# First four weight tiles of an encoder layer regrouped by quarters of the contraction, and the row statistics moved to ScalarE

## The chip, the cores and the metric

One core of one Trainium2 chip runs the whole program. The number compared is the device time of one execution in microseconds (us). The engines are TensorE (PE, matmuls; its weight loads are listed as PEld), VectorE (DVE), ScalarE (ACT), GpSimd (POOL) and SyncE (SP), which here only issues DMA loads and stores.

## The reference, cut to what matters

One layer of an encoder on 256 tokens of width 2048, in float32. The part that the change touches is its beginning: an RMS norm of x and the first columns of one wide input projection.

```python
def rms_norm(x, g):
    xf = x.astype(jnp.float32)
    y = xf * lax.rsqrt(jnp.mean(xf * xf, axis=-1, keepdims=True) + NORM_EPS)
    return (y * g.astype(jnp.float32)).astype(x.dtype)

h = rms_norm(x, norm_g[l])
proj = h @ w_in[l]              # 2048 x 24576
a_qkv, a_gate, b_in, b_gate, c_qkv, c_gate, merge = jnp.split(proj, SPLITS, axis=-1)
# three branches A (dilated attention), B (long convolutions), C (differential attention),
# each times silu of its gate, projected, merged by sigmoid gates, then one output projection
out = ... branches @ w_proj, merged, @ w_out, final rms_norm
```

## The kernel before, in words

All weights are read once, as a stream of tiles of 128 partitions x 2048 floats (1 MB). One tile is one *unit* of work; `_plan` lists the units in order: sixteen gate units (eight for branch A, eight for B), then convolution columns, attention columns, and so on. A gate unit is 128 output columns of `w_in` with the whole contraction of 2048, which is 16 chunks of 128 rows. A unit gets one accumulator in PSUM (tile `acc`, four buffers), 512 wide: TensorE keeps the weights of a chunk still and moves the 256 tokens past them.

Float32 accuracy is made from a split: every operand is a high part (rounded to fp32r) and a low part (the rest). ScalarE makes the high part (`nc.scalar.copy`, L177), VectorE subtracts it to get the low part (L178); both work on half a weight tile at a time (`split_half`), which gives `hl`, four buffers, two tiles' worth. For each chunk TensorE then issues two matmuls: high weights against [x high, x low] side by side, 512 columns (L705), and low weights against x high, 256 columns (L707). I call the two a *pair*; a gate unit is 16 pairs. `half_b` (L729) and `summed` (L737) add the two halves of the accumulator when the unit is done: ScalarE copies one half out, VectorE adds the other.

The order on each engine is the order in which the code issues (manual schedule), so the loop `for i in range(NU)` fixes it. In round i come the end of the units before (`evs`), the split of tile i+1, the load of tile i+3 (`raw`, three buffers, all on SyncE's queue), and the matmuls of unit i in two halves; between the halves a step of a background task (`step`) may run.

The start is special. x comes in transposed (`xt`, four loads of four chunks each, 512 KB) between the halves of the first weight tile. The norm's factor per token (`rstd`) isn't known yet, so the first sixteen units use x*g without it (`xg`, L268 for the high halves on ScalarE, L269 for the low ones on VectorE), and their results are multiplied by `rstd` at the end (L751). GpSimd squares the four x tiles (L238) and adds them in pairs (L240), VectorE adds the rest (`stats_sum`, L278), one matmul with ones sums over the partitions (`stats_rstd`, L283, between the halves of unit 2), ScalarE takes the root (L285) and VectorE the reciprocal (L286). Before the first data TensorE runs 18 and then 4 matmuls on ones (`warm_up`, L228), with the two products of the bias strips between them (L233). GpSimd issues the loads of the small constants (`const`, L217): two ahead of its squares, ten behind them. In rounds 3 and 4 the results of units 0 and 1, then 2 and 3, are taken out of their accumulators.

Of the kernel before, what the change touches and what calls it, by code (L numbers as in the profile page):

```python
# [10 lines left out]
F32 = mybir.dt.float32  # L11
# [4 lines left out]
S = 256  # L16
# [17 lines left out]
def _plan():  # L34
    """The weight stream: one entry per 128 x 2048 tile."""
# [45 lines left out]


def _stream(w_in, w_proj, w_out):
# [69 lines left out]
def trunk_kernel(ctx: ExitStack, tc: tile.TileContext, A, out, dbg=None):  # L153
# [17 lines left out]
    def split_half(i, h):  # L171
        if i >= NU:
            return
        t = base.tile([128, 2, 1024], F32R, name=f"hl{i}_{h}", tag="hl", bufs=4)
        hl[i, h] = t
        src = raw[i][:, 1024 * h:1024 * h + 1024]
# [12 lines left out]
    # ---------------------------------------------------------------- start  # L189
# [8 lines left out]
    nc.scalar.dma_start(norm_g, A["norm_g"])  # L198
    raw[0] = base.tile([128, 2048], F32, name="raw0", tag="raw", bufs=3)
    xt = []  # L200
    for c in range(4):
        t = k4(f"xt{c}", [128, 4, 256])
        nc.sync.dma_start(t, A["xT"][:, 4 * c:4 * c + 4, :])
        xt.append(t)
        if c in (0, 2):
            h = slice(512 * c, 512 * c + 1024)
            nc.sync.dma_start(raw[0][:, h], A["ws"][0][:, h])
# [11 lines left out]

    oh = slab("oh", [35, 768])  # L220
# [11 lines left out]
    for j in range(2):
        nc.tensor.matmul(ps_strip[:, j, 0:384], tabl, oh[:, 384 * j:384 * j + 384], start=True, stop=True)  # L233
    warm_up(4)
    sq = [k4(f"sq{j}", [128, 4, 256]) for j in range(2)]
    sq += [slab(f"sq{j}", [128, 4, 256]) for j in (2, 3)]
    for c in range(4):
# [10 lines left out]
    ident = const("ident", [128, 128])  # L248
# [10 lines left out]
    # x * g, split; its tokens' scale (rstd) is applied to the first products, and to hT  # L259
    xg = []  # L260
    for c in range(4):
        for k in range(4):
            if k % 2 == 0:
                t = slab(f"xg{c}_{k}", [128, 2, 512], F32R)
                xg.append(t)
            g = norm_g[:, 4 * c + k:4 * c + k + 1]
            o = t[:, k % 2]
            nc.scalar.activation(o[:, 0:256], xt[c][:, k], AF.Copy, scale=g)  # L268
            nc.vector.scalar_tensor_tensor(o[:, 256:512], xt[c][:, k], g, o[:, 0:256].bitcast(F32),  # L269
                                           op0=OP.mult, op1=OP.subtract)  # L270
        if c % 2 == 0:
            split_half(0, c // 2)
# [3 lines left out]
    def stats_sum():  # L276
        for a, b in ((sq[0], sq[2]), (sq[0][:, 0:2], sq[0][:, 2:4]), (sq[0][:, 0], sq[0][:, 1])):
            nc.vector.tensor_tensor(a, a, b, op=OP.add)  # L278
        return sq[0][:, 0]
# [26 lines left out]
    # ------------------------------------------------- bias strips and filters' hidden layer  # L306
# [12 lines left out]
    def sine(ps, j, name):  # L319
        """sin(freq * (ps + b)) with the argument brought into [-pi, pi]."""  # L320
# [31 lines left out]
    # ---------------------------------------------------------------- B: long convolutions  # L352
# [12 lines left out]
    def forward(xh, xl, zname):  # L365
        """[c of even, s of even, c of odd, s of odd] -> [Zr, Zr', S, D]."""
# [54 lines left out]
    def spectra(z, g, nm):  # L421
        """Z, G -> [Pc, Pv, Mc, Mv]."""
# [57 lines left out]
    # ---------------------------------------------------------------- A: dilated attention  # L480
# [71 lines left out]
    # ---------------------------------------------------------------- C: differential attention  # L552
# [103 lines left out]
    # ---------------------------------------------------------------- branches, split for the projections  # L656
# [16 lines left out]
    # ---------------------------------------------------------------- the units of the weight stream  # L673
# [269 lines left out]
    for i in range(NU):  # L943
# [44 lines left out]
        for e in evs:  # L988
            next(e, None)
# [100 lines left out]
```

## Time and profile before

| what | value |
|---|---|
| timed runs | 1432.51, 1432.66, 1433.47 us; median 1432.66 |
| profiled execution, span from first to last instruction | 1432.1 us; no time of its own is listed beside the span |
| TensorE busy | 1415.3 us, 99% |
| VectorE, ScalarE, GpSimd busy | 965.2 us, 730.0 us, 53.1 us |
| mean granted TensorE clock | 0.994 of full |
| DMA | 260.36 MB, mean 182 GB/s |

The busy share is a mean over 1432 us: a few us of waiting in one place hardly show in it. To see them one asks what TensorE waited for, and then for the timeline of that stretch. The granted clock is a share of full speed (1.0 is 2.4 GHz, 0.5 is 1.2 GHz).

### The profile page before, as it was taken

How to read it: one execution, taken by the hardware profiler on the slowest of the kernel's cores; microseconds unless marked ns; L12 is line 12 of the kernel's file. 1: busy time of each engine (PE TensorE's matmuls, PEld its weight loads, DVE VectorE, ACT ScalarE, POOL GpSimd, SP SyncE). 2: the span in 40 equal slices, each digit the busy share in tenths (PEclk: the TensorE clock that was granted, in tenths of full speed). 3: DMA queues.
4: the chain of work that ended last, by engine and by line, in shares of the span. 5: the costliest groups of instructions: out<-in, count | busy, mean ns of one | idle time of the engine just before them, and what ended most of it. 6: DMA issues, size and time to landing. Idle time of an engine off the chain costs nothing.

```text
span 1432.1 us, 20342 instructions
## 1 busy us (share of the span) xinstructions
PE 1415.3 (99%) x8134; PEld 1239.4 (87%) x8134; DVE 965.2 (67%) x1374; ACT 730.0 (51%) x1150; POOL 53.1 (4%) x74
## 2 busy tenths in 40 slices
PE   7999999999999999999999999999999999999997
PEld 5888899889988888889888888888888888888886
DVE  7787677676766676676655576775666666666554
ACT  4655545444445444454455576775454554545443
POOL 5000000000000000000000000000000000000000
PEclk8999999999999999999999999999999999999999
DMA  7655445454544445554455545444555556554552
GB/s 256 201 187 188 177 178 171 157 186 174 173 176 157 183 175 171 166 180 171 150 189 188 185 169 188 161 174 177 184 198 177 181 200 251 206 191 177 206 192 102
DMA packets 39870, 260.36 MB, mean 182 GB/s; under 512 B 5315, under 2 KB 5342, under 8 KB 10464
## 3 DMA queue, kind: packets, MB, share of 16 engines
q1 hardware_dynamic: 34992, 246.43, 48.0%
q0 software_dynamic: 4064, 11.58, 3.3%
q8 instruction: 64, 1.05, 0.3%
q10 hardware_dynamic: 720, 1.06, 0.2%
q14 instruction: 30, 0.25, 0.0%
HBM read 256.85 MB, written 2.20 MB: 181 GB/s over the span
## 4 chain that ended last, share of the span: by engine, by line
PE 98%; DVE 1%; DMA 1%; issue 0%; ACT 0%; SPq 0%; DVEq 0%
PE acc L705 48%; PE acc L707 24%; PE acc L722 6%; PE acc L723 6%; PE acc L721 6%; DMA xt<-in_xT 1%; PE ps_ef L407 1%; PE ps_o L473 0%; PE av L546 0%; PE lg L502 0%; DVE xg L269 0%; PE ps_fZ L356 0%; PE ps_fZ L355 0%; PE ps_fG L355 0%; PE ps_fZ L354 0%
## 5 line engine op out<-in xcount | busy, mean ns | idle before, releaser
L705 PE MATMUL acc<-hT,hl 128*128 128x512 f32 x2304 | 815.3, 397 | 0.0
L178 DVE TENSOR_TENSOR hl<-raw,hl 128x1024 fp32r<-128x1024 f32 x464 | 561.6, 1223 | 147.5 <-ACT hl L177 137.5
L707 PE MATMUL acc<-hT,hl 128*128 128x256 f32 x2304 | 646.3, 280 | 0.0
L705 PEld LDWEIGHTS acc<-hT,hl 128*128 128x128 f32 x2304 | 432.3, 188 | 100.4 <-issue 0.3
L177 ACT CAST hl<-raw 128x1024 fp32r<-128x1024 f32 x464 | 480.1, 1050 | 72.2 <-PE acc L723 51.8
L707 PEld LDWEIGHTS acc<-hT,hl 128*128 128x128 f32 x2304 | 435.4, 189 | 0.4
L729 ACT COPY eb<-acc 128x256 f32<-128x256 f32 x176 | 65.2, 371 | 294.1 <-PE acc L707 292.4
L705 PE MATMUL acc<-bhl,hl 128*128 128x512 f32 x384 | 135.1, 392 | 0.0
L721 PE MATMUL acc<-hl,hT 128*128 128x512 f32 (+1 forms) x320 | 111.3, 348 | 0.0
L722 PE MATMUL acc<-hl,hT 128*128 128x512 f32 (+1 forms) x320 | 111.1, 347 | 0.0
L723 PE MATMUL acc<-hl,hT 128*128 128x512 f32 (+1 forms) x320 | 111.1, 347 | 0.0
L707 PE MATMUL acc<-bhl,hl 128*128 128x256 f32 x384 | 108.4, 282 | 0.0
L705 PE MATMUL acc<-xg,hl 128*128 128x512 f32 x256 | 93.4, 405 | 5.3 <-DVE xg L269 5.3
L705 PEld LDWEIGHTS acc<-bhl,hl 128*128 128x128 f32 x384 | 72.1, 188 | 15.7
L737 DVE TENSOR_TENSOR mg<-acc,eb 128x256 f32<-128x256 f32 x48 | 20.3, 423 | 84.0 <-ACT eb L729 84.0
L707 PE MATMUL acc<-xg,hl 128*128 128x256 f32 x256 | 73.9, 289 | 1.5 <-DVE hl L178 1.5
L707 PEld LDWEIGHTS acc<-bhl,hl 128*128 128x128 f32 x384 | 72.5, 189 | 0.0
L723 PEld LDWEIGHTS acc<-hl,hT 128*128 128x128 f32 x320 | 60.6, 189 | 7.6
L721 PEld LDWEIGHTS acc<-hl,hT 128*128 128x128 f32 x320 | 60.6, 189 | 7.5
L722 PEld LDWEIGHTS acc<-hl,hT 128*128 128x128 f32 x320 | 60.6, 189 | 7.2
L705 PEld LDWEIGHTS acc<-xg,hl 128*128 128x128 f32 x256 | 49.8, 194 | 17.6 <-DVE xg L269 4.8
L707 PEld LDWEIGHTS acc<-xg,hl 128*128 128x128 f32 x256 | 50.1, 196 | 2.0 <-DVE hl L178 2.0
(306 smaller groups left out, 1282.3 us busy)
## 6 DMA issues: line engine op xcount, KB each, us to landing
raw<-in_ws SPq DMA_DIRECT2D x229, 1024.0 KB, 4.8
raw<-in_ws SPq DMA_DIRECT2D x6, 512.0 KB, 10.2
xt<-in_xT SPq DMA_DIRECT2D x4, 512.0 KB, 8.1
w<-in_w POOLq DMA_DIRECT2D x8, 256.0 KB, 5.0
xres<-in_x POOLq DMA_DIRECT2D x4, 512.0 KB, 8.9
ab<-strips POOLq DMA_DIRECT2D x8, 192.0 KB, 4.0
cb<-strips POOLq DMA_DIRECT2D x8, 192.0 KB, 3.9
ab<-strips POOLq DMA_DIRECT2D x8, 128.0 KB, 5.0
```

The costliest lines, as they stand in the source:

```text
L177: nc.scalar.copy(t[:, 0], src)
L178: nc.vector.tensor_tensor(t[:, 1], src, t[:, 0].bitcast(F32), op=OP.subtract)
L407: nc.tensor.matmul(ps[:, tt], hidHL[:, 128 * tt:128 * tt + 128], wh[:, j], start=j == 0, stop=j == 1)
L705: nc.tensor.matmul(acc, t[:, 0, 128 * j:128 * j + 128], m, start=first and j == 0, stop=False)
L707: nc.tensor.matmul(acc[:, 0:256], t[:, 1, 128 * j:128 * j + 128], m[:, 0:256], start=False, stop=last and j == 7)
L721: nc.tensor.matmul(o, xh, wh, start=kt == 0, stop=False)
L722: nc.tensor.matmul(o, xh, wl, start=False, stop=False)
L723: nc.tensor.matmul(o, xl, wh, start=False, stop=kt == KT - 1)
L729: nc.scalar.copy(t, acc[:, 256:512])
L737: nc.vector.tensor_tensor(dst, acc[:, 0:256], eb, op=OP.add)
```

## The change

Three things are done. First, tiles 0 to 3 are packed anew: tile q holds contraction chunks 4q to 4q+3 of all four units 0 to 3, instead of all chunks of one unit. TensorE walks through four accumulators per tile, and each accumulator is complete only after tile 3. Loads and splits of the first tile are cut finer, and x is loaded and split chunk by chunk beside the tile that needs it. Second, the squares leave GpSimd: x is loaded a second time in token-major form (`tok`, four tiles of 512 KB), ScalarE squares it with a running sum, and two transposes bring the sums over the tokens into a row. They stand behind the last product of tile 3. Third, some small things move: the strips' products go behind the first half of tile 1, the second warm-up goes, the constants are issued in one go, norm_g goes to SyncE's queue, and results of the first units are taken out one round later (units 0 and 1 in round 4; 2, 3 and 4 in round 5), as are the background steps.

```diff
+NS = 4
 def _stream(w_in, w_proj, w_out):
+    for q in range(NS):
+        dst = ws[q].reshape(128, NS, 4, 128)
+        for j in range(NS):
+            c = UNITS[j]["c"]
+            dst[:, j] = wi[4 * q:4 * q + 4, :, c:c + 128].transpose(1, 0, 2)
...
-    nc.scalar.dma_start(norm_g, A["norm_g"])
+    nc.sync.dma_start(norm_g, A["norm_g"])
...
+    for j in range(2):
+        load_x(0, 2 * j, 2 * j + 2)
+        c = slice(512 * j, 512 * j + 512)
+        nc.sync.dma_start(raw[0][:, c], A["ws"][0][:, c])
+    nc.sync.dma_start(raw[0][:, 1024:2048], A["ws"][0][:, 1024:2048])
     for i in (1, 2):
+        load_x(i)
         load(i)
+    load_x(3)
...
-    warm_up(18)
+    for j in range(16):
+        nc.tensor.matmul(wps, ones, ones, start=j == 0, stop=j == 15)
...
-    for c in range(4):
-        nc.gpsimd.tensor_tensor(sq[c], xt[c], xt[c], op=OP.mult)
-    for c in (0, 2):
-        nc.gpsimd.tensor_tensor(sq[c], sq[c], sq[c + 1], op=OP.add)
...
+    split_x(0)
+    split_part(0, 0, slice(0, 512))
+    for k in (1, 2, 3):
+        split_x(k)
+    split_part(0, 0, slice(512, 1024))
+    split_half(0, 1)
...
+    def stats_load(j):
+        tok[j] = k4(f"tok{j}", [128, 1024])
+        nc.sync.dma_start(tok[j], A["x"][j // 2][:, 1024 * (j % 2):1024 * (j % 2) + 1024])
+
+    def stats_square(j):
+        nc.scalar.activation(tok[j], tok[j], AF.Square, accum_out=sq[:, j // 2, j % 2:j % 2 + 1])
+
-    def stats_rstd(tot):
+    def stats_rstd():
+        tot = base.tile([128, 2], F32, name="tot")
+        nc.vector.tensor_tensor(tot, sq[:, :, 0], sq[:, :, 1], op=OP.add)
         pst = psum.tile([128, 256], F32, name="pst", tag="pa")
-        nc.tensor.matmul(pst, ones, tot, start=True, stop=True)
+        for m in range(2):
+            nc.tensor.transpose(pst[:, 128 * m:128 * m + 128], tot[:, m:m + 1].to_broadcast([128, 128]), ident)
...
     def mm_unit(i, h, ms=(0, 1)):
+        if i < NS:
+            for j in (2 * h, 2 * h + 1):
+                if i == 0:
+                    acc_of[j] = new_acc(j)
+                acc = acc_of[j]
+                for k in range(4):
+                    c = slice(512 * (j % 2) + 128 * k, 512 * (j % 2) + 128 * k + 128)
+                    m = xg[2 * i + k // 2][:, k % 2]
+                    nc.tensor.matmul(acc, t[:, 0, c], m, start=i == 0 and k == 0, stop=False)
+                    nc.tensor.matmul(acc[:, 0:256], t[:, 1, c], m[:, 0:256],
+                                     start=False, stop=i == NS - 1 and k == 3)
...
-        if i < 3:
+        if i < NS:
             evs = []
-        elif i < 5:
-            evs = [2 * (i - 3), 2 * (i - 3) + 1]
+        elif i == NS:
+            evs = [0, 1]
+        elif i == NS + 1:
+            evs = [2, 3, 4]
...
+        if i < NS - 1:
+            for k in range(4 * i + 4, 4 * i + 8):
+                split_x(k)
         split_half(i + 1, 0)
...
         load(i + 3)
+        if i in (0, 1):
+            stats_load(2 * i)
+            stats_load(2 * i + 1)
+        if i in (2, 3):
+            stats_square(2 * i - 4)
+            stats_square(2 * i - 3)
...
         mm_unit(i, 0)
-        if i == 2:
-            stats_rstd(total_sq)
+        if i == 1:
+            strip_products()
...
-        if i == 1:
-            total_sq = stats_sum()
+        if i == NS - 1:
+            stats_rstd()
```

TensorE's first products, before. A name such as acc0 is unit 0's accumulator, xg0 to xg3 are the chunks of x*g by load, hl0_0 and hl0_1 are the halves of split tile 0; in square brackets the engines that an instruction waits for.

```order
L228 MATMUL wps_97<-ones_68 128x128 x4
L705 MATMUL acc0_0_220<-xg0_0_159,hl0_0_169 128x512 [waits DVE_49,Activation_49]
L707 MATMUL acc0_0_220<-xg0_0_159,hl0_0_169 128x256 [waits DVE_49]
L705 MATMUL acc0_0_220<-xg0_0_159,hl0_0_169 128x512
L707 MATMUL acc0_0_220<-xg0_0_159,hl0_0_169 128x256
L705 MATMUL acc0_0_220<-xg0_2_164,hl0_0_169 128x512
L707 MATMUL acc0_0_220<-xg0_2_164,hl0_0_169 128x256
L705 MATMUL acc0_0_220<-xg0_2_164,hl0_0_169 128x512
L707 MATMUL acc0_0_220<-xg0_2_164,hl0_0_169 128x256
L705 MATMUL acc0_0_220<-xg1_0_172,hl0_0_169 128x512 [waits DVE_49]
```

The same place now; here xg0 and xg1 are the first two pairs of chunks.

```order
L718 MATMUL acc0_0_196<-xg1_144,hl0_0_153 128x512 [waits DVE_49]
L719 MATMUL acc0_0_196<-xg1_144,hl0_0_153 128x256
L718 MATMUL acc1_0_205<-xg0_143,hl0_0_153 128x512 [waits Activation_49]
L719 MATMUL acc1_0_205<-xg0_143,hl0_0_153 128x256 [waits DVE_49]
L718 MATMUL acc1_0_205<-xg0_143,hl0_0_153 128x512
L719 MATMUL acc1_0_205<-xg0_143,hl0_0_153 128x256
L718 MATMUL acc1_0_205<-xg1_144,hl0_0_153 128x512
L719 MATMUL acc1_0_205<-xg1_144,hl0_0_153 128x256
```

Before, the fifth pair already needed the second load of x; now the fifth pair goes to the next accumulator with the chunks of the first load, and waits for weights.

TensorE around the statistics (pst), before:

```order
L707 MATMUL acc2_0_305<-xg1_2_177,hl2_0_253 128x256
L283 MATMUL pst_322<-sq0_123,ones_68 128x256 [waits DVE_49,PE_49]
L705 MATMUL acc2_0_305<-xg2_0_182,hl2_1_256 128x512 [waits Activation_49]
L707 MATMUL acc2_0_305<-xg2_0_182,hl2_1_256 128x256
L705 MATMUL acc2_0_305<-xg2_0_182,hl2_1_256 128x512
```

And now, at the end of tile 3:

```order
L718 MATMUL acc3_0_223<-xg7_150,hl3_1_297 128x512
L719 MATMUL acc3_0_223<-xg7_150,hl3_1_297 128x256
L304 MATMUL pst_380<-ident_95,tot_378 128x128 [waits DMASW0_49,DVE_49,PE_49]
L304 MATMUL pst_380<-ident_95,tot_378 128x128
L737 MATMUL acc4_0_405<-xg0_143,hl4_0_336 128x512 [waits DVE_49]
L739 MATMUL acc4_0_405<-xg0_143,hl4_0_336 128x256
```

The statistics moved from the middle of unit 2 to the end of tile 3, and unit 4's first product follows them with a wait for VectorE.

What VectorE did with the results of units 0 and 1, before (rstd is the reciprocal, br the gate's result, eb the half that ScalarE copied out):

```order
L178 TENSOR_TENSOR hl3_1_300<-raw3_218,hl3_1_300 128x1024 [waits Activation_49]
L286 RECIPROCAL rstd_206<-std_324 128x256 [waits Activation_49]
L737 TENSOR_TENSOR br0_0_343<-acc0_0_220,eb0_344 128x256 [waits Activation_49]
L751 TENSOR_TENSOR br0_0_343<-br0_0_343,rstd_206 128x256 [waits DVE_49]
L737 TENSOR_TENSOR br0_0_343<-acc1_0_261,eb1_348 128x256 [waits Activation_49]
L751 TENSOR_TENSOR br0_0_343<-br0_0_343,rstd_206 128x256 [waits DVE_49]
L178 TENSOR_TENSOR hl4_0_352<-raw4_259,hl4_0_352 128x1024 [waits DMAHW4_49,PE_49,Activation_49]
```

And now:

```order
L186 TENSOR_TENSOR hl4_1_339<-raw4_246,hl4_1_339 128x1024 [waits Activation_49]
L301 TENSOR_TENSOR tot_378<-sq_169 128x2 [waits Activation_49]
L307 RECIPROCAL rstd_168<-std_383 128x256 [waits Activation_49]
L769 TENSOR_TENSOR br0_0_386<-acc0_0_196,eb0_387 128x256 [waits PE_49,Activation_49]
L783 TENSOR_TENSOR br0_0_386<-br0_0_386,rstd_168 128x256 [waits DVE_49]
L769 TENSOR_TENSOR br0_0_386<-acc1_0_205,eb1_391 128x256 [waits PE_49,Activation_49]
L783 TENSOR_TENSOR br0_0_386<-br0_0_386,rstd_168 128x256 [waits DVE_49]
L186 TENSOR_TENSOR hl5_0_395<-raw5_300,hl5_0_395 128x1024 [waits DMAHW4_49,Activation_49]
```

The sum that reads unit 0's accumulator (L737 before, L769 now, acc0) stands behind the reciprocal in both. Before, the split of tile 4 followed these results; now that of tile 5 does.

## Rows read from the trace of the kernel before

**Rows 1.** The page's busy time: engine, us, share, instructions.
```profile
PE 1415.3 (99%) x8134; PEld 1239.4 (87%) x8134; DVE 965.2 (67%) x1374; ACT 730.0 (51%) x1150; POOL 53.1 (4%) x74
```
**Rows 2.** TensorE's waits, whole run: total us, times, longest.
```profile
PE acc L705 <- DVE xg L269: 5.3, 4, 1.6
PE acc L707 <- DVE hl L178: 1.5, 1, 1.5
```
**Rows 3.** TensorE's timeline: start us, us, instruction, [idle before <- releaser].
```profile
11.28 0.47 PE L705 MATMUL acc<-xg,hl 128*128 128x512 f32 x1
...
14.04 0.50 PE L705 MATMUL acc<-xg,hl 128*128 128x512 f32 x1 [0.78 <-DVE xg L269]
...
16.07 0.80 PE L705 MATMUL acc<-xg,hl 128*128 128x512 f32 x1 [1.42 <-DVE xg L269]
...
23.39 0.58 PE L707 MATMUL acc<-xg,hl 128*128 128x256 f32 x1 [1.47 <-DVE hl L178]
...
28.89 0.63 PE L705 MATMUL acc<-xg,hl 128*128 128x512 f32 x1
...
29.53 0.43 PE L705 MATMUL acc<-xg,hl 128*128 128x512 f32 x1
...
45.97 0.39 PE L705 MATMUL acc<-xg,hl 128*128 128x512 f32 x1
```
**Rows 4.** Groups by line: 9.9 to 22.1, 22.3 to 25.1, 0 to 46 us.
```profile
L269 DVE SCALAR_TENSOR_TENSOR xg<-xt,norm_g,xg 128x256 fp32r<-128x256 f32 x8 | 12.3, 1604 | 0.0
...
L269 DVE SCALAR_TENSOR_TENSOR xg<-xt,norm_g,xg 128x256 fp32r<-128x256 f32 x4 | 1.7, 472 | 0.0
...
L238 POOL TENSOR_TENSOR sq<-xt 128x1024 f32<-128x1024 f32 x4 | 8.2, 2075 | 5.0 <-DMA xt<-in_xT 5.0
```
**Rows 5.** Stretches: length, busy of PE, PEld, DVE, ACT, POOL, clock, DMA.
```profile
8.00:9.00 1.00, 0.01 (x1) 0.04 (x2) 0.52 (x2) 0.66 (x1) 0.00 (x0) 1.00 1.02 406
...
16.00:17.00 1.00, 0.93 (x2) 0.50 (x2) 1.00 (x2) 1.00 (x2) 1.00 (x1) 0.50 0.73 299
...
29.00:30.00 1.00, 1.00 (x6) 0.86 (x6) 0.43 (x1) 0.53 (x1) 0.00 (x0) 0.71 1.35 135
```
**Rows 6.** Loads issued at 0.74 and 3.56, the chain's wait, one stretch.
```profile
xt<-in_xT SPq DMA_DIRECT2D x1, 512.0 KB, 4.0
...
1.66 7.67 DMA xt<-in_xT
...
xt<-in_xT SPq DMA_DIRECT2D x1, 512.0 KB, 9.5
...
10.00:15.00 5.00, 3.87 (x22) 2.71 (x20) 5.00 (x3) 5.00 (x12) 5.00 (x3) 1.00 1.03 419
```
**Rows 7.** GpSimd's first late constant, and the two largest: KB, us to landing.
```profile
20.67 0.55 POOL L217 DMA_DIRECT2D w<-in_w  x1
...
dft<-in_dft POOLq DMA_DIRECT2D x1, 256.0 KB, 2.9
...
idft<-in_idft POOLq DMA_DIRECT2D x1, 256.0 KB, 6.0
```
**Rows 8.** Groups by line, 0 to 46 us, and L905 from the whole run.
```profile
L178 DVE TENSOR_TENSOR hl<-raw,hl 128x1024 fp32r<-128x1024 f32 x10 | 12.0, 1218 | 3.5 <-ACT hl L177 3.5
L177 ACT CAST hl<-raw 128x1024 fp32r<-128x1024 f32 x10 | 10.4, 1045 | 15.3 <-PE acc L707 14.4 <-DMA raw<-in_ws 0.9
...
L268 ACT ACTIVATE xg<-xt,norm_g 128x256 fp32r<-128x256 f32 x16 | 6.7, 495 | 3.0 <-DMA norm_g<-in_norm_g 2.3 <-DMA xt<-in_xT 0.7
...
L233 PE MATMUL ps_strip<-oh,tabl 35*32 35x384 f32 x4 | 1.4, 481 | 1.4 <-DMA tabl<-in_tabl 1.4
...
L905 ACT ACTIVATE fsq<-xres 128x512 f32<-128x512 f32 x6 | 3.8, 633 | 19.6 <-DVE xres L904 15.7 <-issue 3.9
```
**Rows 9.** Timeline around the statistics: start us, us, instruction.
```profile
37.20 0.59 PE L283 MATMUL pst<-sq,ones 128*128 128x256 f32 x2
...
38.34 1.75 DVE L286 RECIPROCAL rstd<-std 128x256 f32<-128x256 f32 x1 [1.40 <-ACT std L285]
...
40.01 0.36 DVE L737 TENSOR_TENSOR br<-acc,eb 128x256 f32<-128x256 f32 x1
```

More of the change, by code (lines that the diff above doesn't have):

```diff
@@ L165, in load @@
             raw[i] = base.tile([128, 2048], F32, name=f"raw{i}", tag="raw", bufs=3)
-            n = 2 if i < 3 else 1
+            n = 2 if i < NS else 1
             for h in range(n):
@@ L169, in load, with split_part, split_half @@
                 nc.sync.dma_start(raw[i][:, c], A["ws"][i][:, c])
[L171 to L176, printed above, removed]
+    def split_part(i, h, c):
+        if (i, h) not in hl:
+            hl[i, h] = base.tile([128, 2, 1024], F32R, name=f"hl{i}_{h}", tag="hl", bufs=4)
+        t = hl[i, h][:, :, c]
+        src = raw[i][:, 1024 * h:1024 * h + 1024][:, c]
         nc.scalar.copy(t[:, 0], src)
         nc.vector.tensor_tensor(t[:, 1], src, t[:, 0].bitcast(F32), op=OP.subtract)
+    def split_half(i, h):
+        if i < NU:
+            split_part(i, h, slice(0, 1024))
     def k1(name):
@@ L197, in trunk_kernel, with load_x @@
     norm_g = base.tile([128, KT], F32, name="norm_g")
-    nc.scalar.dma_start(norm_g, A["norm_g"])
+    nc.sync.dma_start(norm_g, A["norm_g"])
     raw[0] = base.tile([128, 2048], F32, name="raw0", tag="raw", bufs=3)
-    xt = []
-    for c in range(4):
[L202 to L207, printed above, removed]
+    xt = [k4(f"xt{c}", [128, 4, 256]) for c in range(4)]
+    def load_x(c, k0=0, k1=4):
+        nc.sync.dma_start(xt[c][:, k0:k1], A["xT"][:, 4 * c + k0:4 * c + k1, :])
+    for j in range(2):
[3 more added lines that the diff above has]
+    nc.sync.dma_start(raw[0][:, 1024:2048], A["ws"][0][:, 1024:2048])
     for i in (1, 2):
+        load_x(i)
         load(i)
+    load_x(3)
     nc.scalar.activation(warm, eps, AF.Sqrt)
@@ L218, in const @@
         return t
+    ident = const("ident", [128, 128])
     oh = slab("oh", [35, 768])
@@ L224, in trunk_kernel, with strip_products @@
     wps = psum.tile([128, 128], F32, name="wps", tag="pa")
-    def warm_up(n):
-        for j in range(n):
-            nc.tensor.matmul(wps, ones, ones, start=j == 0, stop=j == n - 1)
-    warm_up(18)
+    for j in range(16):
+        nc.tensor.matmul(wps, ones, ones, start=j == 0, stop=j == 15)
     ps_strip = psum.tile([32, 2, 512], F32, name="ps_strip", tag="pb")
[L232 to L237, printed above, removed]
-        nc.gpsimd.tensor_tensor(sq[c], xt[c], xt[c], op=OP.mult)
-    for c in (0, 2):
-        nc.gpsimd.tensor_tensor(sq[c], sq[c], sq[c + 1], op=OP.add)
+    def strip_products():
+        for j in range(2):
+            nc.tensor.matmul(ps_strip[:, j, 0:384], tabl, oh[:, 384 * j:384 * j + 384],
+                             start=True, stop=True)
     w1 = const("w1", [33, 128], tag="k1")
@@ L247, in trunk_kernel @@
     idft = const("idft", [128, 4, 128])
-    ident = const("ident", [128, 128])
     convw = const("convw", [128, 24, 3])
@@ L257, in trunk_kernel, with split_x @@
         convraw.append(t)
[L260 to L272, printed above, removed]
+    xg = [slab(f"xg{j}", [128, 2, 512], F32R) for j in range(8)]
+    def split_x(k):
+        g = norm_g[:, k:k + 1]
+        o = xg[k // 2][:, k % 2]
+        x = xt[k // 4][:, k % 4]
+        nc.scalar.activation(o[:, 0:256], x, AF.Copy, scale=g)
+        nc.vector.scalar_tensor_tensor(o[:, 256:512], x, g, o[:, 0:256].bitcast(F32),
+                                       op0=OP.mult, op1=OP.subtract)
+    split_x(0)
[4 more added lines that the diff above has]
+    split_half(0, 1)
     hT = base.tile([128, KT, 512], F32R, name="hT")
     rstd = base.tile([128, 256], F32, name="rstd")
[L276 to L279, printed above, removed]
-    def stats_rstd(tot):
+    sq = base.tile([128, 2, 2], F32, name="sq")
+    tok = {}
+    def stats_load(j):
[6 more added lines that the diff above has]
+        nc.vector.tensor_tensor(tot, sq[:, :, 0], sq[:, :, 1], op=OP.add)
         pst = psum.tile([128, 256], F32, name="pst", tag="pa")
-        nc.tensor.matmul(pst, ones, tot, start=True, stop=True)
+        for m in range(2):
+            nc.tensor.transpose(pst[:, 128 * m:128 * m + 128], tot[:, m:m + 1].to_broadcast([128, 128]), ident)
         std = k1("std")
@@ L688, in mm_unit @@
         t = hl[i, h]
-        if u["lay"] in "bp":
+        if i < NS:
[9 more added lines that the diff above has]
+                                     start=False, stop=i == NS - 1 and k == 3)
+        elif u["lay"] in "bp":
             if u["lay"] == "p":
@@ L1000, in trunk_kernel @@
         mm_unit(i, 0)
-        if i == 2:
-            stats_rstd(total_sq)
+        if i == 1:
+            strip_products()
         late = [q for q in "ab" if place[q] == "late"]
-        if i > 2:
+        if i > NS - 1:
             for q in "ab":
```

2 lines of the change are left out of this document (added).

## The prediction, made before the changed kernel was run

> **What bounds the kernel now.** I read the busy shares first, then the waits of TensorE, then its timeline, then the rows of whoever it waits for. TensorE is busy 99% of the 1432.1 us [rows 1]; what it waits for inside its main products adds up to 6.8 us (5.3 for VectorE's low halves of x*g, 1.5 for a low half of weights) [rows 2]. All of it lies before 24 us, so only the start can be won. A product is a pair of matmuls (512 columns, then 256). Five pairs run close together from 11.28, and then each waits alone, at 14.04, 16.07 and twice more, until the rest of the first tile runs in one piece from 23.39 [rows 3]. The pair at 29.53 is the 19th, and the 22 pairs from there to the statistics' matmul at 37.20 take 0.349 us each [rows 3, 9]. Eighteen pairs at 0.349 are 6.3 us of work, and they took 18.25: 12 us are lost between 11.28 and 29.53, besides the time before 11.28.
>
> Two things made that loss. VectorE's low halves of x*g took 1604 ns each between 9.9 and 22.1 us, while GpSimd squared x (2075 ns a tile), and 472 ns once it had finished [rows 4]. And the granted clock went from full to half (2.4 to 1.2 GHz) around 16 us, after the waits before 14.04 and 16.07, and came back between 29 and 30, after matmuls without a gap since 23.39 [rows 5]. At half clock a pair takes 0.64 us (28.89 to 29.53) [rows 3].
>
> The last mark I need is 45.97: there unit 4, the fifth gate tile, starts (24 pairs of unit 2 and 3 follow the statistics' matmul at 37.20) [rows 3, 9]. From there on both kernels issue the same products, apart from a few background steps that come one unit later, with 12 units until their results are needed; so the change is worth 45.97 minus the time at which its unit 4 starts.
>
> **The change, part by part.**
>
> *First tiles.* Sixteen pairs now need four chunks of x instead of sixteen, and the four tiles are still 64 pairs, 64 x 0.349 = 22.3 us. When the data come: before, the first 512 KB of SyncE's queue landed at 0.74 + 4.0 = 4.7 us, the third at 1.66 + 7.67 = 9.3 and the sixth, issued at 3.56, at 3.56 + 9.5 = 13.1, with 419 GB/s moved between 10 and 15 us [rows 6]. Norm_g is issued ahead of them now (one issue, 0.45 us later). GpSimd's constants, ten loads that started at 20.67 us behind the squares, now go out from about 2 us: dft and idft of 256 KB each and eight small ones, 720 KB in all [rows 7]. At 420 GB/s that is 1.75 us of transfer in a stretch that was already full. I charge it in proportion as it passes: second 512 KB (first quarter of x and half of tile 0 complete) at 8.5, third (the rest of tile 0) 10.4, fourth (x) 12.1, fifth and sixth (tile 1) 13.8 and 15.1.
>
> In the Trainium skill, "DMA: Bandwidth & Descriptors", section "Issuing engines are not separate DMA queues", loads of all issuing engines share the same 16 DMA engines and interleave. That speaks against moving the constants forward; if they cost nothing, tile 1 would be there 1.75 us sooner and the sum below about 1 us smaller. That the moved rate of 419 GB/s did not rise with more queues in use agrees with it, without proving it.
>
> Work on arrival: 1.05 us for ScalarE's cast of half a tile, 1.2 for VectorE's rest, 0.5 or a little less for each chunk of x on either [rows 4, 8]. The warm-up matmuls (16 for 18) end near 7; the first quarter tile is split by 7.3, so I start the products at 7.0. Tile 0's second half: 10.4 + 1.05 + 1.2 = 12.7, then 7.5 pairs: 15.3 instead of 12.6, 2.7 us of waiting. Tile 1: 13.8 + 2.3 = 16.1, another 0.6. Later tiles come faster than they are used: per tile 1.5 MB or 3.75 us of transfer, some 4 us each of ScalarE and VectorE, against 5.6 us of TensorE. Waits 3.3 us; bounds 1.5 (constants free) and 6 (everything 2.5 us later).
>
> *Bias strips.* Their two products stood in the warm-up, where they cost nothing; now they stand between the halves of tile 1, on the path. Four matmuls, 1.4 us with a little overlap [rows 8]: +1.3. If tile 1's second half were late it would be hidden: bounds 0 and 1.4.
>
> *Squares.* Off GpSimd, so VectorE's 1604 ns becomes 472; that is why 4 us a tile holds. On ScalarE a 512-wide square takes 633 ns [rows 8]; for 1024 wide I take twice that, 1.25 us, four times, between the splits. The copies of x are loaded behind tile 3 and tile 4; by 420 GB/s the last lands at 30 and is squared by 32, while tile 3's products end at 7.0 + 22.3 + 3.3 + 1.3 = 33.9. Cost 0, cover 2 us.
>
> *Statistics and the accumulators.* This is the new wait. There are four accumulators, and all four are now in use until tile 3 ends. Unit 4 needs one back: its first matmul waits for VectorE's sum of unit 0, which stands in VectorE's queue behind the reciprocal, which waits for ScalarE's root, which waits for the statistics' transposes, which now stand behind tile 3's last product. Before, the same chain ran from 37.20 to 40.01 + 0.36 = 40.37, of it 1.75 the reciprocal, and TensorE worked beside it on unit 2 and unit 3 [rows 9]. Now it has nothing to do for that 3.2 us. Behind the reciprocal also stand the splits of tile 5, which have 5 us of room. Bounds 3.0 and 3.6.
>
> *The clock after that wait.* No wait in TensorE's list is longer than 1.6 us [rows 2], so its price is bounded by the nearest rows: the clock fell after waits of 0.8 and 1.4 us with one pair between them, and when it was half, 9.6 pairs between 23.39 and 29.53 took 6.1 us instead of 3.35, a price of 2.8 [rows 3, 5]. Ends 0 and 2.8; the new wait is longer than the two that made it fall, so I take 2.0.
>
> In the Trainium skill, "TensorE: Matmul & The Clock Gate", section "HAM oscillation — how this bites in real kernels", every wait of this kind between bursts of matmuls puts the engine back to half clock for the start of the next burst. By it the 2.0 is due in each execution; without it the time would be 1423.9.
>
> *Sum.* 7.0 + 22.3 + 3.3 + 1.3 + 3.2 + 0.1 (release) = 37.2, and 45.97 - 37.2 = 8.8 us gained; minus 2.0 for the clock, 6.8. The profiled span of 1432.1 becomes 1425.3; the median of the timed runs lies 0.56 above that span, which I leave as it is: 1432.66 - 6.8 = 1425.9.
>
> **The rivals.**
>
> 1. *The clock holds* in both places: the gain is 8.8, 1423.9; with the constants free, near 1422. For: the warm-up leaves it full, and the us from 8 to 9, with almost no matmul, did not make it fall [rows 5]. Against: the wait at unit 4 is three times that.
> 2. *The clock also falls in tile 0 or 1*, since waits of 0.5 to 0.9 us stand between the quarter tiles, like those before 14.04. Price up to another 2.8, part of it inside waits for data: gain 4.0 to 5.5, about 1428.
> 3. *The change does little of what it says*: the start is bound by the loads, not by VectorE. If each landing is 2.5 us later than I have it, waits are 6 us, and with both falls of the clock the gain is 1.5 to 2.8: 1430.5.
> 4. *Slower: the statistics come late.* Every us that the fourth square is later than 33.9 is a us of TensorE idle, since all four accumulators are held. The last two copies of x wait for the first two squares and stand in SyncE's queue behind tile 4's load. The longest landing of the x rows is 9.5 us [rows 6]: issued at 25, landed at 34.5, squared by 37, 3.2 us lost and still a gain of 3.6. It turns the sign when the last square ends 8.8 - 2.0 = 6.8 us later than 33.9, near 41, which takes a landing of some 13 us; then 1433, and beyond 1435.5 it is measurably slower.
>
> **How the numbers follow.** Likeliest forecast (1424.8 to 1427.2) 0.45, rival 1 0.25, rival 2 0.18, rival 3 0.08, rival 4 0.04. For eight times in ten I leave out the best end of rival 1 and most of rivals 3 and 4: 1422.0 to 1430.0. A difference under 0.2% (2.9 us) can't be told from none here, so faster means under 1429.8: the forecast, rival 1 and nearly all of rival 2, 0.86; same 0.10 from the rest of rival 2, rival 3 and part of rival 4; slower 0.04.
>
> **What would show it.** Right: the first product near 7 us; low halves of x*g at 472 ns throughout; one TensorE wait of 3.2 us before unit 4, ended by VectorE's sum of unit 0, and half clock behind it; unit 4 at 37 us. Wrong: a wait for squares ahead of the transposes; first landings more than 2 us off; a wait after unit 4, which would mean that the background steps do matter; unit 4 at 37 and yet less than 5 us gained.

## The result, and the profile after

The changed kernel takes 1425.01 us (median of 5 runs, 1424.31 to 1425.53) against 1433.47 (1432.51 to 1433.72) on the same chip: a ratio of 0.9942, 95% interval 0.993 to 0.9954. 1425.9 was forecast. The agreement is partly luck: the start gave about 4.4 us and not 6.8, and another 4.1 us came from something the prediction didn't have. Experiments 5 to 8 separate the two.

The page first, against [rows 1]: the span is 8.9 us shorter, and TensorE is as full as before.

```profile
span 1423.2 us, 20340 instructions
...
PE 1408.4 (99%) x8122; PEld 1235.7 (87%) x8122; DVE 953.6 (67%) x1373; ACT 734.7 (52%) x1159; POOL 40.1 (3%) x68
```

TensorE's waits in the first 46 us (total us, times, longest), against [rows 2]. Those for low halves of x*g (5.3 us before) are gone; one for VectorE's sum of unit 0 (L769) and one ahead of the statistics' transposes (L304) are new.

```profile
PE acc L737 <- DVE br L769: 2.6, 1, 2.6
PE acc L719 <- DVE hl L186: 1.7, 3, 0.8
...
PE pst L304 <- PE acc L719: 1.0, 1, 1.0
PE acc L718 <- ACT hl L185: 0.6, 2, 0.4
```

TensorE's timeline, against [rows 3, 9] (start us, us, instruction, idle before and releaser; L718 and L719 are a pair of the first four tiles, L737 opens a pair of the later ones).

```profile
7.25 0.48 PE L718 MATMUL acc<-xg,hl 128*128 128x512 f32 x1
...
12.87 0.38 PE L719 MATMUL acc<-xg,hl 128*128 128x256 f32 x1 [0.75 <-DVE hl L186]
...
15.40 0.28 PE L719 MATMUL acc<-xg,hl 128*128 128x256 f32 x1
16.04 0.50 PE L718 MATMUL acc<-xg,hl 128*128 128x512 f32 x1 [0.35 <-ACT hl L185]
17.30 0.39 PE L719 MATMUL acc<-xg,hl 128*128 128x256 f32 x1 [0.76 <-DVE hl L186]
...
20.04 1.47 PE L248 MATMUL ps_strip<-oh,tabl 35*32 35x384 f32 x4
21.44 0.50 PE L718 MATMUL acc<-xg,hl 128*128 128x512 f32 x1
...
35.30 0.28 PE L719 MATMUL acc<-xg,hl 128*128 128x256 f32 x1
...
36.56 0.40 PE L304 MATMUL pst<-ident,tot 128*128 128x128 f32 x2 [0.99 <-PE acc L719]
...
39.60 0.50 PE L737 MATMUL acc<-xg,hl 128*128 128x512 f32 x1 [2.63 <-DVE br L769]
```

Tile 0 ends about 15.5, tile 1's halves are separated by the strips, tiles 2 and 3 run without a gap to about 35.5, and unit 4 starts at 39.60, where before it started at 45.97: 6.4 us sooner, not 8.8.

VectorE's low halves of x*g in the first tiles (7 to 30 us), against [rows 4]: 481 ns, no longer 1604.

```profile
L276 DVE SCALAR_TENSOR_TENSOR xg<-xt,norm_g,xg 128x256 fp32r<-128x256 f32 x15 | 6.4, 481 | 0.5 <-ACT xg L275 0.5
```

The chain between tile 3 and unit 4, all engines (SPq is SyncE's queue). The releaser named at 36.56 was done at 35.6; what came last is the fourth square, which had waited 2.03 us for its copy of x. The two last copies had themselves waited for buffers that the first two squares set free (first line, from the queue's waits: total us, times, longest), and went out at 27.44 and 28.68; the second landed 6.4 us later.

```profile
SPq L294 <- ACT tok L297: 9.5, 2, 8.6
...
27.44 1.57 SPq L294 DMA_DIRECT2D tok<-in_x  x2
...
35.12 1.06 ACT L297 ACTIVATE tok<-tok 128x1024 f32<-128x1024 f32 x1 [2.03 <-DMA tok<-in_x]
...
36.30 0.16 DVE L301 TENSOR_TENSOR tot<-sq 128x2 f32<-128x2 f32 x1 [2.82 <-ACT tok L297]
...
37.01 0.47 ACT L306 ACTIVATE std<-pst,eps 128x256 f32<-128x256 f32 x1 [0.73 <-PE pst L304]
...
37.51 1.75 DVE L307 RECIPROCAL rstd<-std 128x256 f32<-128x256 f32 x1 [1.05 <-ACT std L306]
...
39.18 0.36 DVE L769 TENSOR_TENSOR br<-acc,eb 128x256 f32<-128x256 f32 x1
```

The granted clock, against [rows 5] (length, busy time of PE, PEld, DVE, ACT, POOL, clock, DMA share, GB/s): full in tiles 0 and 1, half behind the wait ahead of unit 4, full again from 44.

```profile
8.00:9.00 1.00, 1.00 (x5) 0.69 (x6) 0.79 (x2) 0.27 (x1) 0.54 (x1) 1.00 1.03 379
16.00:17.00 1.00, 0.50 (x1) 0.19 (x1) 0.98 (x1) 0.96 (x1) 0.00 (x0) 1.00 1.02 418
40.00:41.00 1.00, 1.00 (x7) 0.92 (x6) 0.97 (x4) 0.85 (x3) 0.00 (x0) 0.84 0.22 90
41.00:42.00 1.00, 1.00 (x4) 0.81 (x4) 0.93 (x1) 1.00 (x2) 0.00 (x0) 0.50 0.09 33
...
44.00:45.00 1.00, 1.00 (x7) 0.88 (x7) 0.97 (x3) 0.00 (x0) 0.00 (x0) 0.95 0.67 164
```

The surprise lies behind all that. The 6.4 us at unit 4 less about 1.6 for the clock are 4.8, and the span is 8.9 shorter. Between two given interludes of background matmuls lie 48 pairs of the same products in both kernels; hT is the normed x, which all units behind the first sixteen use. These are their first and last 512-column matmuls, before and then after.

```profile
593.59 0.40 PE L705 MATMUL acc<-hT,hl 128*128 128x512 f32 x1
...
610.20 0.40 PE L705 MATMUL acc<-hT,hl 128*128 128x512 f32 x1
```

```profile
586.72 0.40 PE L737 MATMUL acc<-hT,hl 128*128 128x512 f32 x1
...
603.02 0.39 PE L737 MATMUL acc<-hT,hl 128*128 128x512 f32 x1
```

The 47 pitches take 16.61 us before and 16.30 after, 353 and 347 ns each, with no wait in either. The lead is 6.9 us at this place, where it was 4.8 behind unit 4.

### The profile page after: what moved, and what is told of

It reads as the page before. It is cut to its first block, busy times and chain, and to the rows that moved or that the text cites. A ratio compares the mean times of both kernels' runs of the same rounds, so it can differ in the third digit from the quotient of the medians.

```text
span 1423.2 us, 20340 instructions
## 1 busy us (share of the span) xinstructions
PE 1408.4 (99%) x8122; PEld 1235.7 (87%) x8122; DVE 953.6 (67%) x1373; ACT 734.7 (52%) x1159; POOL 40.1 (3%) x68
## 4 chain that ended last, share of the span: by engine, by line
PE 98%; DMA 1%; DVE 0%; issue 0%; SPq 0%; ACT 0%; DVEq 0%
PE acc L737 47%; PE acc L739 24%; PE acc L755 6%; PE acc L753 6%; PE acc L754 6%; PE acc L718 1%; DMA raw<-in_ws 1%; PE ps_ef L428 1%; PE ps_o L494 1%; PE av L567 1%; PE lg L523 1%; PE acc L719 0%; PE ps_fG L376 0%; PE ps_fG L375 0%; PE ps_fZ L377 0%; PE ps_fG L377 0%
## 5 line engine op out<-in xcount | busy, mean ns | idle before, releaser
L737 PE MATMUL acc<-hT,hl 128*128 128x512 f32 x2304 | 810.5, 395 | 0.0
L186 DVE TENSOR_TENSOR hl<-raw,hl 128x1024 fp32r<-128x1024 f32 (+1 forms) x465 | 562.0, 1221 | 153.1 <-ACT hl L185 143.2
L737 PEld LDWEIGHTS acc<-hT,hl 128*128 128x128 f32 x2304 | 431.9, 187 | 96.8 <-issue 0.3
L185 ACT CAST hl<-raw 128x1024 fp32r<-128x1024 f32 (+1 forms) x465 | 480.3, 1049 | 61.7 <-PE acc L755 50.9
L737 PE MATMUL acc<-bhl,hl 128*128 128x512 f32 x384 | 135.4, 393 | 0.0
L737 PEld LDWEIGHTS acc<-bhl,hl 128*128 128x128 f32 x384 | 72.1, 188 | 16.1
L769 DVE TENSOR_TENSOR mg<-acc,eb 128x256 f32<-128x256 f32 x48 | 20.3, 423 | 84.2 <-ACT eb L761 84.2
L737 PE MATMUL acc<-xg,hl 128*128 128x512 f32 x192 | 68.4, 398 | 2.6 <-DVE br L769 2.6
L739 PE MATMUL acc<-xg,hl 128*128 128x256 f32 x192 | 54.9, 286 | 0.0
L755 PE MATMUL acc<-hl,yhl 128*128 128x512 f32 x128 | 50.5, 395 | 0.0
L754 PE MATMUL acc<-hl,yhl 128*128 128x512 f32 x128 | 50.5, 395 | 0.0
```

Source lines behind the costliest of these rows:

```text
L737: nc.tensor.matmul(acc, t[:, 0, 128 * j:128 * j + 128], m, start=first and j == 0, stop=False)
L739: nc.tensor.matmul(acc[:, 0:256], t[:, 1, 128 * j:128 * j + 128], m[:, 0:256], start=False, stop=last and j == 7)
L754: nc.tensor.matmul(o, xh, wl, start=False, stop=False)
L755: nc.tensor.matmul(o, xl, wh, start=False, stop=kt == KT - 1)
L769: nc.vector.tensor_tensor(dst, acc[:, 0:256], eb, op=OP.add)
```

## The experiments

**1. Two warm-up matmuls fewer** (kernel before): is the pace a matter of TensorE's instruction count?

```
-    warm_up(18)
+    warm_up(16)
```

> The kernel before with 16 instead of 18 matmuls in the first warm-up, nothing else. TensorE waits from 7.5 to 9.0 us there anyway, so by the start alone the time is unchanged. What it tests is the second half of the gain: of the 8.9 us of span that the changed kernel saves, only 4.8 are there at 105 us; the other 4.1 come between 200 and 960 us, where pairs of matmuls take 353 ns in one kernel and 347 in the other. Theory A (the pace is a state that TensorE falls into after a background step, by its exact timing or place in the instruction stream): the stretches at 353 and 347 ns lie elsewhere than before, and the total can move by up to 4 us either way. Theory B (the pace comes from which buffers lie where, or from work that the change took off GpSimd): the buffers and the work are as before, so the time is that of before within 0.6 us.

1432.73 us against 1432.80, ratio 1.0001 (0.9992 to 1.001). The pace of every stretch stayed as it was (the count under experiments 7 and 8 is the same, 2574). So it doesn't depend on this count of instructions.

**2. Squares alone** (kernel before, without the new layout): token-major copies squared on ScalarE, statistics behind unit 2.

```
-    for c in range(4):
-        nc.gpsimd.tensor_tensor(sq[c], xt[c], xt[c], op=OP.mult)
...
+    sq = base.tile([128, 2, 2], F32, name="sq")
...
+        if i in (0, 1):
+            stats_load(2 * i)
+            stats_load(2 * i + 1)
+        if i in (1, 2):
+            stats_square(2 * i - 2)
+            stats_square(2 * i - 1)
```

> One part alone: the squares on ScalarE from a token-major copy, in the tile layout of before; the statistics follow unit 2. If VectorE's slow low halves (1604 ns beside GpSimd's squares) made the loss, and not the layout, the low halves take about 472 ns, tile 0 is done near 17 us and unit 4 starts at 35 to 38 us, earlier than in the changed kernel (39.6), since an accumulator is free: at the start 8 to 11 us faster than before. If the layout made the gain, tile 0 is still late and unit 4 starts after 41 us. The pace of later stretches adds between 0 and 4 us of gain in either case.

1424.54 us, ratio 0.9946 (0.9931 to 0.996): as much as the whole change. In its waits (as above) nothing is left of x*g; there are accumulators free, and the statistics' chain has products beside it. The 1.4 us ahead of the transposes (L284) are listed without a releaser; the total before them had waited 1.59 us for the last square, so here too the squares came late.

```profile
PE pst L284 <- issue: 1.4, 1, 1.4
...
PE acc L708 <- DVE hl L178: 0.4, 1, 0.4
```

The filters' first matmul, at the same place of the program in both, starts at 96.69 instead of 104.30 (this kernel, then before), 7.6 us sooner; the other 1.8 of its 9.4 us of span come later.

```profile
96.69 0.48 PE L338 MATMUL ps_h<-zT,w 33*128 33x256 f32 x1
```

```profile
104.30 0.48 PE L337 MATMUL ps_h<-zT,w 33*128 33x256 f32 x1
```

**3. Layout alone** (changed kernel with the squares on GpSimd again, and the addresses of before, see 5).

```
+    for c in range(4):
+        nc.gpsimd.tensor_tensor(sq[c], xt[c], xt[c], op=OP.mult)
...
-        if i in (0, 1):
-            stats_load(2 * i)
-            stats_load(2 * i + 1)
...
+        if i == NS - 2:
+            total_sq = stats_sum()
```

> The other part alone: the changed layout, with the squares on GpSimd as before. VectorE's low halves of x*g go back to about 1600 ns while GpSimd works. Theory squares: tiles 1 to 3 are late by 16 low halves x 1.1 us less the cover, unit 4 starts at 43 to 46 us, with the wait for the accumulators on top (3 us): no faster than before at the start. Theory layout: each tile needs four low halves only, 6.4 us against 5.6 of matmuls, so unit 4 starts at about 41 us.

1432.55 us, ratio 0.9998 (0.9989 to 1.0007): no gain that can be measured. The low halves are slow again (GpSimd's squares, now 2437 ns, stand beside them), and the wait for unit 0's sum is there too. Unit 4 starts at 43.17, where the theory of the squares had it at 43 to 46 and that of the layout at about 41.

```profile
L282 DVE SCALAR_TENSOR_TENSOR xg<-xt,norm_g,xg 128x256 fp32r<-128x256 f32 x12 | 15.9, 1374 | 0.0
```

```profile
PE acc L717 <- DVE hl L186: 3.8, 3, 2.3
PE acc L735 <- DVE br L767: 2.6, 1, 2.6
PE acc L716 <- DVE xg L282: 1.6, 1, 1.6
```

**4. Sums of units 0 to 3 ahead of the statistics** (changed kernel; the transposes behind the first half of unit 4). gate_sum adds the two halves of a unit's accumulator into br; rstd and the gate follow a unit later.

```
+        if i == NS - 1:
+            gate_sum(0, UNITS[0])
+            gate_sum(1, UNITS[1])
+            stats_square(3)
+        if i == NS:
+            stats_rstd()
...
-            stats_rstd()
+            gate_sum(2, UNITS[2])
+            gate_sum(3, UNITS[3])
```

> The changed kernel with the sums of units 0 to 3 taken out of their accumulators ahead of the statistics (they don't need them), and the statistics' transposes behind the first half of unit 4. If the wait of unit 4 is the accumulators held behind the reciprocal, TensorE's waits of 1.0 and 2.6 us vanish, unit 4 starts right behind tile 3 at 35.5 instead of 39.6, the clock doesn't fall (1.6 us): 5.7 us less, about 1419.3, if the pace of later stretches stays as in the changed kernel; 4 us more if it goes back. Rival: unit 5 waits instead, for its split behind the squares (1 to 2 us), and 1421.

1423.63 us (1422.36 to 1424.33), ratio 0.9938 (0.9922 to 0.9955): neither the 1419.3 nor the rival's 1421. The wait kept its 2.6 us and went to another place: unit 4 starts at 35.60 at once, and in its middle TensorE waits for the total, which stands on VectorE behind two splits.

```profile
PE pst L304 <- DVE tot L301: 2.6, 1, 2.6
```

Next, two kernels in which every instruction is the same and only addresses in SBUF move.

**5. Kernel before, with the offsets of after.**

```
+    ident = base.tile([128, 128], F32, name="ident")
     oh = slab("oh", [35, 768])
...
-    ident = const("ident", [128, 128])
+    nc.gpsimd.dma_start(ident, A["ident"])
...
-    rstd = base.tile([128, 256], F32, name="rstd")
+    rstd = base.tile([128, 264], F32, name="rstd")[:, 0:256]
...
-    nlam = base.tile([128, 1], F32, name="nlam")
+    nlam = base.tile([128, 16], F32, name="nlam")[:, 0:1]
```

> The kernel before, with the same instructions; only addresses in SBUF move, to the offsets that the changed kernel has: the identity's tile is laid out ahead of the one-hot table (so all buffers behind it, the slabs and the small ones, lie 512 bytes further on), rstd's tile is 32 bytes longer and nlam's as well (so what follows lies 32 and 64 bytes further on). The slabs are handed out in the order of before. Theory A (the offsets decide which of its two paces TensorE takes in the products of hT): the start is that of before (statistics' matmul near 37.2, unit 4 near 46.0), the pairs at 444 to 451 us take 346.7 ns instead of 353.3, and the span falls by what the changed kernel gained there, 4 us or a little less: 1428.6 us, 1428 to 1429.5. Theory B (which slab a tile gets, or the times of the other engines): 1432.7 and 353.3 ns there, as before.

1428.70 us against 1433.02, ratio 0.997 (0.9958 to 0.9981): 4.3 us from addresses alone.

**6. Changed kernel, with the offsets of before.** The small tiles sq and tot, which the change adds, go into a tile that exists, and ident behind idft.

```
-    sq = base.tile([128, 2, 2], F32, name="sq")
+    sq = warm[:, 1:5].rearrange("p (m c) -> p m c", m=2)
...
-        tot = base.tile([128, 2], F32, name="tot")
+        tot = warm[:, 5:7]
```

> The changed kernel, with the same instructions; only addresses in SBUF move, back to the offsets of before: the identity's tile behind idft, the squares' sums and their total in eight columns of a tile that is there already. Slabs and k4 buffers are handed out as in the changed kernel. Theory A (offsets decide the pace): unit 4 still starts near 39.6, the pairs at 438 to 444 us take 353.3 ns, and 4.1 of the 8.4 us gained are lost: 1429.1, 1428.3 to 1430. Theory B (the slabs' order or the times of other engines): 1425.0, as the changed kernel.

1428.65 us, ratio 0.9967 (0.9954 to 0.9979). Of the 8.5 us that the change gained, 4.4 are left. The same 48 pairs, in this kernel, take 16.60 us again. The profile is of the quickest of the five executions (1427.17), in which unit 4 starts at 38.92: 7.0 us sooner than in the kernel before, 6.8 sooner at these 48 pairs, and the span is 6.7 shorter. So behind the start nothing more is gained here, where the changed kernel gained another 4.

```profile
38.92 0.50 PE L744 MATMUL acc<-xg,hl 128*128 128x512 f32 x1 [2.63 <-DVE br L776]
...
586.77 0.40 PE L744 MATMUL acc<-hT,hl 128*128 128x512 f32 x1
...
603.37 0.40 PE L744 MATMUL acc<-hT,hl 128*128 128x512 f32 x1
```

**7 and 8. Which offset?** Kernel before, with each half of experiment 5's edit by itself: ident's 512 bytes, or the 32 bytes each of rstd and nlam.

> The kernel before with the first of the two shifts alone: the identity's tile laid out ahead of the one-hot table, so that the slabs and the 1 KB buffers (operands of most background matmuls) lie 512 bytes further on; k4 buffers and the rest stay. Theory A1 (the slabs' offset decides the pace): all or nearly all of the 4.3 us that both shifts gave, 1428.5 to 1429.5, and 346.7 ns a pair at 444 to 451 us. Theory A2 (the 32 and 64 bytes decide): 1432.5 to 1433.3, and 353.3 ns there.

> The kernel before with the second shift alone: rstd's and nlam's tiles 32 bytes longer, so that the split filters lie 32 bytes and the eb and k4 buffers 64 bytes further on; slabs stay. Theory A1 (the slabs decide): 1432.5 to 1433.3, 353.3 ns a pair at 444 to 451 us. Theory A2: 1428.5 to 1429.5 and 346.7 ns there.

512 bytes: 1432.77 us, ratio 0.9998 (0.9989 to 1.0006). 32 and 64 bytes: 1428.64 us, ratio 0.9969 (0.9956 to 0.9981), all of the gain. The same 48 pairs with 512 bytes, and then with 32 and 64:

```profile
591.67 0.40 PE L706 MATMUL acc<-hT,hl 128*128 128x512 f32 x1
...
608.28 0.40 PE L706 MATMUL acc<-hT,hl 128*128 128x512 f32 x1
```

```profile
590.19 0.40 PE L705 MATMUL acc<-hT,hl 128*128 128x512 f32 x1
...
606.49 0.39 PE L705 MATMUL acc<-hT,hl 128*128 128x512 f32 x1
```

16.61 and 16.30. The place that the expectations named, 444 to 451 us, was badly chosen: with 512 bytes it is quick as well, since that shift made some stretches quick and others slow. Over the whole trace, of all triples of hT's pairs (three pairs in a row are six steps, counted from each matmul), so many took 1060 ns and not 1040, each within some 8 ns; a surplus of 20 ns over six steps makes the last row.

| | before | 512 bytes | 32 and 64 | both | after | after, offsets of before |
|---|---|---|---|---|---|---|
| 1060 ns | 2574 | 2495 | 1369 | 1278 | 1255 | 2628 |
| 1040 ns | 1395 | 1469 | 2598 | 2683 | 2712 | 1345 |
| us lost to it | 8.6 | 8.3 | 4.6 | 4.3 | 4.2 | 8.8 |

The differences in the last row are near those of the medians: 4.0 us for 32 and 64 bytes (4.6 by the times), 4.3 for both (4.3), and 4.6 between the last two columns (4.1, as 8.5 less 4.4).

**9. Sums early, statistics behind the whole of unit 4** (changed kernel with experiment 4's edit; what is shown is the edit against that).

```
-        if i == NS:
-            stats_rstd()
...
-        if i > NS - 1:
+        if i > NS:
...
+        if i == NS:
+            stats_rstd()
```

> The changed kernel with the sums of units 0 to 3 taken out of their accumulators as soon as tile 3 ends, and the statistics' transposes behind the whole of unit 4 (the background steps start one unit later). Theory: nothing is left for TensorE to wait for between tile 3 and unit 6, so of the 3.6 us that it lost there (1.0 ahead of the transposes, 2.6 ahead of unit 4) and the 1.6 at half clock behind it about 5 come back, less what tile 4's split costs: 1420 to 1421, unit 4 at about 36.3. Rival: VectorE and ScalarE, with four sums to do before the next splits, become late with tile 5, and the wait turns up there: 1423 to 1425.

1419.63 us (1419.15 to 1420.35), ratio 0.9906 (0.9891 to 0.9921). Unit 4 starts at 35.86, and TensorE doesn't wait in it; the clock stays full. What is left are the waits of tiles 0 and 1.

```profile
PE acc L719 <- DVE hl L186: 1.7, 3, 0.8
...
PE acc L718 <- DVE xg L276: 0.8, 1, 0.8
```

**10. Strips between the halves of tile 0** (changed kernel).

```
-        if i == 1:
+        if i == 0:
             strip_products()
```

> The changed kernel with the strips' two products between the halves of tile 0, where TensorE waits 0.75 us, instead of between those of tile 1. Theory A (TensorE's own work sets the end of tile 3, as the prediction had it): unit 4 starts about 1.3 us sooner than 39.6, and the time is 1423.7. Theory B (the fourth square ends at 36.2 whatever TensorE does, and the statistics' chain runs from there): tile 3 ends near 34, the wait ahead of the transposes grows from 1.0 to 2.3, unit 4 starts at 39.6 still and the time is 1425.0.

1424.97 us, but scattered (1422.44 to 1426.25). The median says that nothing was gained, as expected if the fourth square sets the end. The profile is of the quickest execution, and its copy of x landed sooner: the square runs at 32.78 instead of 35.12, and unit 4 starts at 37.27. From the end of the accumulator's read to unit 4 it is 3.33 us there (33.94 to 37.27) and 3.33 in the changed kernel (36.27 to 39.60). So unit 4 follows the fourth square, and that follows a load.

```profile
32.78 1.06 ACT L297 ACTIVATE tok<-tok 128x1024 f32<-128x1024 f32 x1 [0.37 <-DMA tok<-in_x]
33.75 0.19 ACT L297 ACTIVATION_READ_ACCUMULATOR tok<-tok 128x1 f32 x1
```

**11. Experiment 9 with the strips in tile 0.**

> The version with the early sums and the statistics behind unit 4 (1419.63), and the strips' two products between the halves of tile 0. Theory: with the fourth square off the path, TensorE's own work and tile 1's loads set the end of tile 3; the strips fill the 0.75 us that TensorE waits in tile 0, and what they push further is taken back in tile 1's waits (0.35 and 0.76): 1.2 to 1.4 us less, 1418.3. Rival: the second half of tile 1 then waits for its own load, and nothing is gained: 1419.6.

1419.44 us (1419.07 to 1419.63): nothing that can be told from 1419.63, though not by the rival's way. Unit 4 starts 1.9 us sooner, at 33.97, and gives 0.9 of it back to the statistics, whose total still stands behind the splits.

```profile
PE pst L304 <- DVE tot L301: 0.9, 1, 0.9
```

**12. The same, with GpSimd's constants from w1 on held back.**

```
+    nc.gpsimd.tensor_copy(warm, xt[2][:, 3, 255:256])
     w1 = const("w1", [33, 128], tag="k1")
```

> As the run with early sums and strips in tile 0, and GpSimd's constants from w1 on (about 530 KB) held back until the third chunk of x has landed. Theory A (as the prediction charged them, in proportion to the bytes): 530 KB at 420 GB/s are 1.3 us, the waits in tiles 0 and 1 (2.5 us in all) shrink by about 1 us, 1417.3. Theory B (the constants ride along at no cost): 1418.3.

1417.72 us, the best median, ratio 0.9896 (0.9883 to 0.991); its four runs reach from 1416.63 to 1421.32, so the 1.7 us below experiment 11 are not settled. The loads are held back as meant (nine of 656 KB in all, not the 530 of the expectation), and what they made room for is plain: the median landing of the 512 KB weight loads issued in the first 15 us (KB each, us to landing), in experiment 11 and then here.

```profile
raw<-in_ws SPq DMA_DIRECT2D x7, 512.0 KB, 11.0
```

```profile
raw<-in_ws SPq DMA_DIRECT2D x7, 512.0 KB, 8.8
```

## Why the prediction came out right, and where it was wrong

*The squares* were the cause, as it said: 1604 became 481 ns, and experiments 2 and 3 split the change cleanly. Squares alone gain all, the layout alone nothing. The prediction credited the layout with the early products; together with the squares it costs about 2.8 us of the start (7.6 in experiment 2, 4.8 with both), since it holds all four accumulators and leaves the statistics uncovered.

*Products and waits.* Start 7.25 (forecast 7.0). Tile 0 took 2.7 us more than its 16 pairs, as forecast. Tile 1 lost 1.6, not 0.6, because its first half landed at 14.9, issued 4.14, and not at 13.8; the strips cost 1.5 for 1.3. Tile 3 therefore ended at about 35.4 and not at 33.9.

*Squares at no cost, with 2 us of cover.* The square itself was priced right (1.06 and 0.19 for 1.25), its time was wrong: the last copy was to land at 30, and its square ran at 35.12. I priced the load by its bytes, and it is issued only when a buffer is free, at 28.68, then stays in flight for 6.4 us. That cost 1.0 us ahead of the transposes here, and by experiments 10 and 11 it set what other edits were worth. It was rival 4, at a third of its price.

*Statistics and accumulators.* Right in mechanism and size: 3.2 forecast, and 3.0 from the transposes to unit 4 (36.56 to 39.60). Experiments 4 and 9 show that it is the order on VectorE that makes it: sums first takes the wait away once the statistics leave unit 4 as well: the gain over the kernel before grows from 8.5 to 13.4 us, with the 1.0 and the clock in it.

*The clock.* It fell where forecast, 40.7 to 44.1, and cost about 1.6 for 2.0: 3.4 us at 0.64 us a pair, where 0.347 would do. But it doesn't fall in each execution. In experiment 10's profile a wait of 2.63 us halved it again, in experiment 4's a wait of 2.6 us left it full, and in experiment 6's, behind the 2.63 us ahead of 38.92, this row shows it full. The Trainium skill ("TensorE: Matmul & The Clock Gate", section "HAM oscillation — how this bites in real kernels") tells of waits of some 3 to 5 us between bursts of matmuls, each of which put the clock back; of the four waits of about 2.6 us here, two did.

```profile
40.00:41.00 1.00, 1.00 (x8) 0.88 (x6) 1.00 (x2) 0.86 (x3) 0.00 (x0) 1.00 0.14 57
```

*The constants.* They don't ride along at no cost: with 656 KB held back the weights land 2.2 us sooner (11.0 to 8.8), where 656 KB at 420 GB/s are 1.6. So "in proportion" was rather too little, and may be part of why tile 1 came 1.1 us late. It agrees with what the Trainium skill says of queues that share the engines ("DMA: Bandwidth & Descriptors", section "Issuing engines are not separate DMA queues"), and so do the rows above: 379 GB/s from 8 to 9 us with GpSimd's loads in flight, 418 from 16 to 17 behind them. What it is worth in time stayed unsettled.

*The step that failed* is "From there on both kernels issue the same products, apart from a few background steps [...]; so the change is worth 45.97 minus the time at which its unit 4 starts". The products are the same, their pace is not. TensorE runs hT's pairs at 347 or 353 ns, and the change turned 1300 of the triples at 1060 ns into triples at 1040, 4.1 us by the times and 4.4 by the count. Experiment 5 produces this with no other edit, experiment 6 takes it away. Without it the changed kernel takes 1428.65; the forecast's mechanism at the start was right, its term for the start 2.4 us too big, and the two errors met.

A part of those 2.4 us may be the mark 45.97 itself, which is one execution's: in the profiles of experiments 1, 5, 7 and 8, which start as the kernel before does but for two warm-up matmuls in experiment 1, unit 4 starts at 44.50 to 45.70. Nor is 0.56 the step from span to time. In every run that lists both for one execution it is 1.7 to 1.8 us (1424.94 and 1423.2 here), so the span of 1432.1 belongs to a time of about 1433.8, and not to the 1432.66 that it was set beside.

Left open: why an offset acts on the pace (by the order in which the kernels lay out their tiles, the operands hT and the weights' halves did not move in experiments 5 to 8; no trace shows addresses), and which of the shifts, 32 bytes of the split filters or 64 of eb and the k4 buffers, decides. Experiment 2, where the weights' halves and hT lie 32 bytes further on as well, has a third pattern.

## What to carry to other kernels

When TensorE is full, ask of each new small tile what it pushes along in SBUF: here shifts of 32 and 64 bytes were worth as much as the work on the start, and an edit should be compared with a version of the same addresses before its gain is put down to the edit. A wait is not removed by moving the instruction that shows it; find what stands in front on the releaser's engine (here sums behind a reciprocal, then a total behind splits). A load that waits for a buffer is to be timed from its issue, not from its bytes.

## What the hardware showed that I had not expected

- Two paces of the same products: three pairs in 1040 ns or in 1060 ns, at full clock, with no wait. The pace mostly changes at the interludes of background matmuls, and the pattern repeats from run to run with the same offsets (2574 triples at 1060 ns in the kernel before and in experiment 1).
- A shift of 512 bytes left the time where it was (ratio 0.9998), one of 32 and 64 bytes took 4.6 us off.
- The reader of a square's accumulated sum is an instruction of its own, 0.19 us behind each 1.06 us square.
- A wait of 2.63 us halved the granted clock in one execution and not in another of the same instructions (0.84 and 1.00 in the row from 40 to 41 us).
